# Block 2's scores: a 64-row product for q's low part, or one of 128 rows with zeros

## The chip, the cores and the metric

One core of one Trainium2 chip. The metric is the device time of one launch in microseconds (us). The kernel before was run three times: median 2690.28 us (2690.26, 2690.28, 2696.82).

## The reference

Two transformer blocks, one after the other, on 256 tokens of 1024 features, all in float32. The change touches the attention scores of the second block alone. There each of two layers has 16 heads of 64 features, in two kinds of eight: neighbourhood heads with a relative bias, and windowed heads that share two heads of keys and have a sink. The stream x (256 tokens) looks at its own 256 keys and at the 256 of the context stream c; in layer 0 the context looks at its own 256 keys. Cut to what matters:

```python
s_nb  = einsum('bqhd,biqjhd->bhqij', q_r, k_win) + bias
s_ctx = einsum('bqhd,bchd->bhqc', q_r, k_ctx)
p     = softmax(concatenate([s_nb, s_ctx]))
out   = p_nb @ v_win + p_ctx @ v_ctx
```

## The kernel before, in words

Features lie on the partitions, tokens along the free dimension. Every large product is made in three: weights and activations are split in a high part of 12 significant bits and the exact rest, and high x high, low x high and high x low are added in one bank of PSUM (`feat`, line 161; each weight unit is loaded by DMA, its high part made by ScalarE (ACT), its low part by VectorE (DVE), `weight`, line 140).

One loop (`main`, line 1462) writes the whole program out: it holds threads (the two streams, their attentions, norms) and always lets the one go on whose next step is ready first, by a clock of its own that `mul` (line 109) moves on by the columns of each product, whatever its rows. TensorE (PE) keeps exactly this order. Where a softmax is not done, the other threads' products stand between, so that TensorE has work.

The scores of block 2 come from `attn2` (line 1280). For each head `make` (line 1289) prepares the operands, one head ahead of its use. `keys` (line 840) writes a tile kk of 128 partitions: the head's 64 rows of k, high part, on its own half (from partition kp) and the low part of the same on the other half. `queries` (line 848) writes a tile qq with two planes: the high part of q on both halves (two casts by ACT, line 852), and the low part on the head's own half alone (a subtraction by GpSimd, POOL, line 854); the other half of the second plane holds nothing. The tiles kk and qq have three buffers each.

`unit` (line 1302) is one query tile of 128 for x (512 keys) or both for c (256 keys each); `DEPTH` = 4 units (line 1543) may be open at a time. Its products are listed at line 1319 and made by `rows_of` (line 640, products at line 651, in the profile under line 110):

```python
jobs.append(([(qh, kk), (ql, kk[kp:kp + 64])], b, init, nm[:, hi, qt:qt + 1], sm[:, hi, qt:qt + 1]))
```

The first product of the pair has 128 rows, high q times both parts of k; the second has the 64 rows of the head, low q times high k. Both add into one bank. Then DVE adds the bias and takes the maximum (line 659), ACT takes the exponential (line 665, followed by a read of its accumulator), TensorE turns the tile with four transposes (`turn`, line 669), DVE or ACT copies it (line 292 or 294), and four products with v follow (`values`, line 679). The neighbourhood heads' bias tile is made by `na_bias` (line 1358) with a memset of 128x256 on GpSimd (line 1362).

Of the kernel before, what the change touches and what calls it, by code (L numbers as in the profile page):

```python
# [10 lines left out]
F32 = mybir.dt.float32  # L11
# [5 lines left out]
OP = mybir.AluOpType  # L17
# [4 lines left out]
D = 1024  # L22
# [10 lines left out]
def rows(ap):  # L33
    """[128, n, 256] -> [128, 2n, 128]"""
    return ap.rearrange("p a (b c) -> p (a b) c", c=128)


def back(ap):
    """the same, the 128 tokens of each tile from the last to the first"""
    return rows(ap)[:, :, ::-1]  # L40


class Late:
    """h = a * x * (its tokens' own scales) + b before those scales are there"""
# [9 lines left out]
class Block:  # L54
    """One launch: both blocks of the reference, features on partitions."""
# [42 lines left out]
    def dma(self, out, in_):  # L98
        """in the order of emission, like the work that frees the tiles"""
        self.nc.sync.dma_start(out, in_)  # L100
# [17 lines left out]
    def lat(self, what):  # L118
        """how long it takes until the tensor engine can go on after..."""
        return LAT["x" if self.phase[0] == "x" else "b"][what]  # L120

    def after(self, us):
        """a thread's request to go on once the tensor engine has had this much other work"""
        return ("at", self.clock + us)

# [4 lines left out]
    def fence(self, ins):  # L130
        """later weights are to be split after this"""
        self.fences[ins.ins.engine] = ins.ins
        self.fenced = 0
# [6 lines left out]
    def weight(self, unit):  # L140
        """unit: (input name, leading indices..., first k-tile, k-tiles). (hi, lo), [128, k-tiles, columns] each"""
        if unit in self.store and self.units - self.store[unit][2] <= HELD:
            return self.store[unit][:2]
        src = self.a[unit[0]]
# [8 lines left out]
        # block 1 has the most for DVE to do  # L153
# [7 lines left out]
    def feat(self, out, w, c0, h, hk, first, last, k0=0, k1=None):  # L161
        """out[feature, token] (+)= sum_k w[k, feature] h[k, token], k0 <= k < k1"""
# [10 lines left out]
    def feats(self, name, blocks, h, parts):  # L173
        """one or two blocks of 128 columns into one bank; a generator that returns the bank"""
# [8 lines left out]
    def burst(self, name, pairs, h, emit):  # L183
        """like feats on up to four pairs of blocks, the first of each together, as the tiles of h come.
        emit(which, bank)"""
# [16 lines left out]
    def early(self, name, pairs, late, emit):  # L202
        """like burst, with the tiles of an h that is not normalised yet: late.u. emit(which, banks, columns), a bank for each
        block; the columns [128, 2] are the products with late.u's last two"""
# [41 lines left out]
    def toks(self, name, b, h):  # L246
        """out[token, feature] for 256 columns; a generator that returns the bank"""
# [15 lines left out]
    def rsqrt(self, v):  # L263
        """1/sqrt of a positive float32 tile: a start from the exponent, a step of the third order (times 8/3), one of
        Newton's"""
# [19 lines left out]
    def spread(self, out, col):  # L285
        """out[p, tok] = col[tok] for every p; col [128 tokens, 1]"""
        self.flop(out, col.to_broadcast([128, 128]))
# [15 lines left out]
    def first_h(self, x, cx, units):  # L303
        """the first scale and shift, and h, two feature tiles at a time as the weights of both come"""
# [82 lines left out]
    def affine_split(self, hh, hl, src, k0, a, b):  # L387
        """h = src * a + b on two feature tiles (src [128, 2, 256]); hi and lo"""
# [15 lines left out]
    def add_to(self, key, src, mp, eng):  # L404
        """running sums of feature tiles, two at a time; the last two are kept as they are"""
# [11 lines left out]
    def feed(self, key, x, mp, sums=False):  # L417
        """feature tiles 2 mp and 2 mp + 1 of x are done: add up their squares, and for a LayerNorm their sums"""
# [9 lines left out]
    def total(self, out, tiles):  # L428
        """out[tok] = mean over the partitions and tiles [128, 128 tok]"""
        for i, t in enumerate(tiles):  # L430
            self.mul(out, t, self.ones, i == 0, i == len(tiles) - 1)

    def late_tile(self, late, x, mp):
        """feature tiles 2 mp and 2 mp + 1 of late.u: x times the norm's and the modulation's factors, without the
        tokens' own, which come later"""
# [16 lines left out]
    def ln_shift(self, x):  # L452
        """move the mean of each token's sum so far out of x, so that the variance is well kept"""
# [20 lines left out]
    def ln_late(self, g, b, sh, sc):  # L474
        """what of LN(x) * g + b and h = that * sc + sh is known before x"""
# [9 lines left out]
    def ln_finish(self, key, x, g, b, late=None):  # L485
        """x = LN(x) * g + b, and h = x * late.a + late.b split"""
# [50 lines left out]
    def rms(self, th, x, a, b, late=None):  # L537
        """h = x * rsqrt(mean(x^2) + eps) * a + b, split"""
# [36 lines left out]
    def ffn(self, tags, h, wi, wo, emit, gate, last_gate=None, th=None):  # L575
        """tags: the pages that the product of gate and up may take; a part of seven pages holds six tiles' hi and lo.
        h: hi and lo, or a Late. gate: the event that emit waits for (last_gate, where it is another in the last part).
        emit(parts left, pair, psum) receives each part of the down product"""
# [4 lines left out]
        for i0 in range(0, FT, per):  # L583
# [30 lines left out]
            for mp in range(4):  # L614
# [3 lines left out]
                if late and mp < 2 and len(parts) == 1:  # L618
                    # the last tile of gf is new: it comes last in both
# [20 lines left out]
    def rows_of(self, jobs):  # L640
        """jobs: ([(q, k [.., keys])], additives, start of -max, -max out, sums out), together at most 512 keys wide.
        exp(the sum of q k + additive - max), queries on the partitions"""
# [26 lines left out]
    def turn(self, e):  # L669
        """e [128 q, n keys] -> [128 keys, n / 128, 128 q]"""  # L670
# [12 lines left out]
    def oturn(self, h, osb, k0, scale=None):  # L683
        """osb [128 tokens from the last, 2 halves, 256 features] -> feature tiles k0, k0 + 1 of h; split"""
# [13 lines left out]
    def normed(self, po, sm):  # L698
        """po [128, 2, 4, 64] / sums [128, 4, 2]"""
# [9 lines left out]
    def attend(self, groups, done, gate=None):  # L709
        """A thread. groups: (units, finish); a unit is a generator that yields how long its next step should wait, or  # L710
        that and True when that step has to come in the order of the units; finish, called after the last unit, is a
        generator too, that starts once the event gate has come. done: the event at the end"""
# [45 lines left out]
    def tables(self):  # L758
        """A thread: [head row, 255 - distance] of additive biases, in DRAM, for Toeplitz reads; the differential lambda"""
# [34 lines left out]
    def project(self, name, h, grp, th):  # L794
        """q, k feature-major pages (q scaled, from the last token), v token-major pages"""
# [39 lines left out]
    def causal_jobs(self, q, k, b, nm, sm):  # L835
        """both query tiles of a head: 128 keys, then 256"""
# [3 lines left out]
    def keys(self, k, p0):  # L840
        """k [64 at p0, n]: its hi there, its lo on the other 64 partitions"""
# [6 lines left out]
    def queries(self, q, p0):  # L848
        """q [64 at p0, n]: its hi on all partitions; its lo, [64 at p0, n]"""
# [3 lines left out]
        lo = qq[p0:p0 + 64, 1, :]  # L853
        self.nc.gpsimd.tensor_tensor(out=lo, in0=q, in1=qq[p0:p0 + 64, 0, :].bitcast(F32), op=OP.subtract)
        return qq[:, 0, :], lo

    def attn_diff(self, box):
        """differential heads, two to a group"""
# [54 lines left out]
    def attn_heads(self, grp, box, k0, bias):  # L913
        """eight causal heads, four to a group; bias(head) -> additive [128, 256]"""
# [34 lines left out]
    def forget(self, h):  # L949
        """log_sigmoid(fd + forget_b) and its running sums"""  # L950
# [18 lines left out]
        # log_sigmoid(x) = min(x, 0) - log1p(exp(-|x|)); log1p(e) = ln(u) e / (u - 1), u = 1 + e  # L969
# [13 lines left out]
        # where u == 1, log1p(e) = e to float32; elsewhere ln(u) e / (u - 1)  # L983
# [7 lines left out]
        # running sums with the tokens on partitions, as they come and turned within each tile  # L991
# [17 lines left out]
    def fox_bias(self, hd):  # L1009
        """cum[q] - cum[k], masked to k <= q; queries 0..127 against keys 0..127 sit in columns 128.."""  # L1010
# [89 lines left out]
    def consts1(self):  # L1100
# [7 lines left out]
        # block 1 needs the one, block 2 the other  # L1108
# [9 lines left out]
    def half_out(self, name, o, k0, emit):  # L1118
        """the product with the feature tiles k0 .. k0 + 3 of o"""
# [11 lines left out]
    def consts2(self):  # L1131
# [16 lines left out]
        # q carries the attention scale  # L1148
# [5 lines left out]
    def head_norm(self, tiles, l, done, turned=None):  # L1154
        """A thread. tiles: list of (AP [128, n, 256], gain index, rotary). In place: x * rsqrt(mean over 64 + eps) * g;
        turned: whether their tokens are from the last. done: the event at the end"""
# [56 lines left out]
    def ffn2(self, th, x, l, s, feed, late=None):  # L1213
        """a half step; the squares of its result are summed for the next norm"""
# [19 lines left out]
    def kv(self, th, h, l):  # L1234
        """k (normed, roped) in feature-major pages shared with the other stream, v token-major"""
# [439 lines left out]
```

## Time and profile before

| What | |
|---|---|
| runs | 2690.26, 2690.28, 2696.82 us |
| profiled execution | span 2698.2 us; the page gives no other time of it |
| mean granted TensorE clock | 0.959 |
| TensorE products, busy | 2577.8 us, 96% of the span |
| VectorE (DVE), busy | 1757.5 us, 65% |
| ScalarE (ACT), busy | 1054.8 us, 39% |
| GpSimd (POOL), busy | 224.6 us, 8% |
| chain that ended last | TensorE 77%, DVE 10%, DMA 6% |

How to read it: all times are from the start of the span. PE is TensorE's products, PEld its weight loads, which can run beside products. Matmuls are pipelined, and their ends are modelled, so the distance from one start to the next tells more than a length. A bracket gives an engine's idle time just before an instruction and what ended it; "issue" is time in which it waited for nothing that the profile shows. The granted clock is 1.00 at the full level (2.4 GHz) and 0.50 at the lower one (1.2 GHz).

### The profile page before, as it was taken

Reading aid. Unit: us, or ns where it says so; the run is one execution under the profiler, and the core shown is the slowest. Engines: PE = TensorE matmul, PEld = TensorE weight load, DVE = VectorE, ACT = ScalarE, POOL = GpSimd, SP = SyncE. Lnnn points to the kernel's source line nnn. Section 1 sums busy time; section 2 is a strip of 40 time slices with the busy share of each in tenths; the row PEclk is TensorE's granted clock in tenths of the full one; section 3 lists DMA queues with packets and bytes.
Section 4 is the critical chain, followed back from the end, with each engine's and each line's share of the span. In section 5 each row is a group of like instructions: output and inputs, shape, how many; then the busy total and the mean of one; then the engine's idle time right before and its main releaser. Section 6 shows DMA issues by size and latency. Waiting matters only on the chain.

```text
span 2698.2 us, 49424 instructions
## 1 busy us (share of the span) xinstructions
PE 2577.8 (96%) x20192; PEld 2491.7 (92%) x20192; DVE 1757.5 (65%) x3392; ACT 1054.8 (39%) x1894; POOL 224.6 (8%) x239
## 2 busy tenths in 40 slices
PE   5989998999998999999999999999999999999999
PEld 4879998989998999999888999999999999987999
DVE  6878886678787655676654765656744545675754
ACT  3545444545443222233555322222322223455543
POOL 1111002120000000001431000000000000041000
PEclk9979997979998999999997999999999999989999
DMA  7866884646763444444210244444443444330554
GB/s 279 268 207 211 286 282 154 202 128 199 244 190 111 152 144 139 143 125 133 82 37 32 85 144 132 157 137 138 137 129 118 147 134 127 126 101 32 172 183 139
DMA packets 127396, 410.55 MB, mean 152 GB/s; under 512 B 15617, under 2 KB 21313, under 8 KB 127041
## 3 DMA queue, kind: packets, MB, share of 16 engines
q1 hardware_dynamic: 127168, 407.40, 47.5%
q8 instruction: 158, 2.59, 0.4%
q14 instruction: 70, 0.57, 0.1%
HBM read 406.27 MB, written 1.07 MB: 151 GB/s over the span
## 4 chain that ended last, share of the span: by engine, by line
PE 77%; DVE 10%; DMA 6%; issue 3%; ACT 3%; POOL 1%; SPq 0%; ACTq 0%; DVEq 0%; POOLq 0%
PE ps_mm L110 64%; PE ps_s L110 4%; PE ps_o L110 4%; PE ps_t L115 3%; DVE wl L128 3%; DMA raw<-in_w_ffn_in 2%; PE ps_t L110 2%; DVE junk L376 2%; DMA adaw<-in_w_ada 2%; ACT wh L128 1%; DMA raw<-in_w_ffn_out 1%; DVE x_res L636 1%; DMA raw<-in_w_o 1%; POOL tr L394 0%; DVE tr L563 0%
## 5 line engine op out<-in xcount | busy, mean ns | idle before, releaser
L110 PE MATMUL ps_mm<-hh,wh 128*128 128x256 f32 (+1 forms) x3968 | 1146.6, 289 | 38.7 <-ACT hh L392 23.0
L110 PE MATMUL ps_mm<-hl,wh 128*128 128x256 f32 (+1 forms) x3968 | 1135.9, 286 | 8.0 <-DVE hl L396 4.8
L110 PE MATMUL ps_mm<-hh,wl 128*128 128x256 f32 (+1 forms) x3968 | 1137.0, 287 | 2.1 <-DVE wl L128 2.1
L128 ACT CAST wh<-raw 128x1024 fp32r<-128x1024 f32 (+2 forms) x574 | 547.8, 958 | 756.4 <-PE ps_mm L110 473.8
L110 PEld LDWEIGHTS ps_mm<-hh,wh 128*128 128x128 f32 x3968 | 769.3, 194 | 49.2 <-ACT hh L392 23.4
L128 DVE TENSOR_TENSOR wl<-raw,wh 128x1024 fp32r<-128x1024 f32 (+2 forms) x558 | 627.8, 1129 | 259.3 <-ACT wh L128 256.5
L110 PEld LDWEIGHTS ps_mm<-hl,wh 128*128 128x128 f32 x3968 | 767.8, 193 | 11.9 <-DVE hl L396 5.6
L110 PEld LDWEIGHTS ps_mm<-hh,wl 128*128 128x128 f32 x3968 | 768.6, 194 | 2.6 <-DVE wl L128 2.5
L376 DVE SCALAR_TENSOR_TENSOR junk<-adaw,cb 128x1024 fp8e4<-128x1024 f32 x344 | 426.0, 1238 | 25.2 <-DMA adaw<-in_w_ada 21.6
L110 PE MATMUL ps_mm<-x,wh 128*128 128x256 f32 x1704 | 332.5, 284 | 1.7 <-DVE x_res L636 1.7
L110 PEld LDWEIGHTS ps_mm<-x,wh 128*128 128x128 f32 x1704 | 275.8, 191 | 2.4 <-issue 1.7
L110 PE MATMUL ps_mm<-c,wh 128*128 128x256 f32 x1376 | 269.9, 284 | 3.5 <-ACT c L128 2.2
L595 DVE TENSOR_TENSOR tr<-tr,ps_mm 128x256 f32<-128x256 f32 x189 | 79.3, 420 | 253.8 <-ACT tr L594 252.8
L110 PE MATMUL ps_mm<-x,wl 128*128 128x256 f32 x852 | 241.8, 284 | 1.2 <-DVE wl L128 1.2
L594 ACT ACTIVATE tr<-ps_mm 128x256 f32<-128x256 f32 x189 | 72.6, 384 | 430.2 <-PE ps_mm L110 429.7
L110 PEld LDWEIGHTS ps_mm<-c,wh 128*128 128x128 f32 x1376 | 222.6, 190 | 4.7 <-ACT c L128 2.4
L110 PE MATMUL ps_mm<-c,wl 128*128 128x256 f32 x688 | 194.9, 283 | 1.4 <-DVE wl L128 1.4
L110 PEld LDWEIGHTS ps_mm<-x,wl 128*128 128x128 f32 x852 | 162.7, 191 | 1.4 <-DVE wl L128 1.4
L1187 POOL COPY tr<-small 128x256 f32<-128x256 f32 x44 | 21.0, 507 | 1386.7 <-DVE small L282 1353.2
L110 PEld LDWEIGHTS ps_mm<-c,wl 128*128 128x128 f32 x688 | 130.9, 190 | 1.6 <-DVE wl L128 1.6
L636 DVE SCALAR_TENSOR_TENSOR c_res<-ps_mm,ada_c,c_res 128x256 f32<-128x256 f32 x112 | 49.3, 479 | 93.0 <-PE ps_mm L110 93.0
L665 ACT ACTIVATE e<-e,small 128x512 f32<-128x512 f32 (+2 forms) x160 | 90.7, 568 | 42.9 <-DVE small L659 40.4
(254 smaller groups left out, 2784.9 us busy)
## 6 DMA issues: line engine op xcount, KB each, us to landing
adaw<-in_w_ada SPq DMA_DIRECT2D x232, 512.0 KB, 4.3
raw<-in_w_ffn_up SPq DMA_DIRECT2D x176, 512.0 KB, 3.8
raw<-in_w_ffn_in SPq DMA_DIRECT2D x88, 512.0 KB, 4.5
raw<-in_w_ffn_down SPq DMA_DIRECT2D x96, 384.0 KB, 3.2
raw<-in_w_ffn_out SPq DMA_DIRECT2D x48, 384.0 KB, 3.9
raw<-in_w_in SPq DMA_DIRECT2D x28, 512.0 KB, 3.8
raw<-in_w_in_ab SPq DMA_DIRECT2D x16, 512.0 KB, 6.4
raw<-in_w_o SPq DMA_DIRECT2D x16, 512.0 KB, 4.8
```

The costliest lines, as they stand in the source:

```text
L110: self.tc.keep_in_program_order(self.nc.tensor.matmul(out, left, right, start=start, stop=stop))
L115: self.tc.keep_in_program_order(self.nc.tensor.transpose(out, in_, self.ident))
L128: return (self.nc.scalar.copy(hi, src), (eng or self.nc.vector).tensor_tensor(out=lo, in0=src, in1=hi.bitcast(F32), op=OP.subtract))
L376: ins = self.nc.vector.scalar_tensor_tensor(out=self.junk, in0=raw, scalar=1.0, in1=v, op0=OP.mult, op1=OP.mult, accum_out=acc[:, j:j + 1] ...
L594: nc.scalar.activation(sg[:, 0, :], ps[:, 0, :], AF.Silu)
L595: nc.vector.tensor_tensor(out=sg[:, 1, :], in0=sg[:, 0, :], in1=ps[:, 1, :], op=OP.mult)
L636: self.nc.vector.scalar_tensor_tensor(out=x[:, k, :], in0=ps[j], scalar=gate[:, k:k + 1], in1=x[:, k, :], op0=OP.mult, op1=OP.add)
L665: nc.scalar.activation(e[:, at:at + w], e[:, at:at + w], AF.Exp, bias=nm, scale=-1.0, accum_out=sm)
L1187: nc.gpsimd.tensor_copy(wide, r[:, :, i, :, None].to_broadcast([128, 2, 2, 64]))
```

## The change

`queries` writes zeros to the other half of the second plane, with a memset on GpSimd ahead of the subtraction, and returns the whole plane. The second product of each pair takes all 128 rows of it with the whole of kk: low q times high k on the head's half, zero times low k on the other. Everything else in the diff takes out comments and moves no code.

```diff
     def queries(self, q, p0):
         qq = self.page("qq", (128, 2, q.shape[1]), F32R)
         for p in (p0, 64 - p0):
             self.nc.scalar.copy(qq[p:p + 64, 0, :], q)
-        lo = qq[p0:p0 + 64, 1, :]
-        self.nc.gpsimd.tensor_tensor(out=lo, in0=q, in1=qq[p0:p0 + 64, 0, :].bitcast(F32), op=OP.subtract)
-        return qq[:, 0, :], lo
+        self.nc.gpsimd.memset(qq[64 - p0:128 - p0, 1, :].bitcast(F32), 0.0)
+        self.nc.gpsimd.tensor_tensor(out=qq[p0:p0 + 64, 1, :], in0=q, in1=qq[p0:p0 + 64, 0, :].bitcast(F32),
+                                     op=OP.subtract)
+        return qq[:, 0, :], qq[:, 1, :]
...
     def attn2(self, th, l, box, kind):
...
-                jobs.append(([(qh, kk), (ql, kk[kp:kp + 64])], b, init, nm[:, hi, qt:qt + 1], sm[:, hi, qt:qt + 1]))
+                jobs.append(([(qh, kk), (ql, kk)], b, init, nm[:, hi, qt:qt + 1], sm[:, hi, qt:qt + 1]))
```

## Rows read from the trace of the kernel before

**Rows 1.** The chain of waits, 1290 to 1490 us, its shares by line

```profile
by line: PE ps_mm L110 29.2%; PE ps_o L110 25.0%; PE ps_s L110 23.7%; PE ps_t L115 17.2%; PE ps_t L110 2.7%; DVE e L659 0.7%; DVE junk L376 0.5%; DVE hl L128 0.3%; DVE pt L292 0.3%; issue 0.3%; DVE small L1177 0.1%; DVE small L702 0.1%; DVE
```

**Rows 2.** Windows, all engines: start:end, length, busy us (count), granted clock, DMA

```profile
1300.00:1490.00 190.00, 187.81 (x1158) 159.62 (x1157) 105.54 (x273) 105.24 (x261) 55.04 (x74) 0.86 0.13 41
2390.00:2490.00 100.00, 93.99 (x605) 74.86 (x604) 61.60 (x139) 57.12 (x127) 28.54 (x34) 0.95 0.16 48
```

**Rows 3.** Groups by form, low products and their weight loads: busy, mean; idle, releasers

```profile
L110 PE MATMUL ps_s<-kk,qq 64*128 64x512 f32 x64 | 33.3, 520 | 0.0
...
L110 PEld LDWEIGHTS ps_s<-kk,qq 64*128 64x128 f32 x96 | 19.1, 199 | 21.6 <-issue 18.3 <-POOL tr L1187 0.3 <-POOL qq L854 0.2
...
L110 PE MATMUL ps_s<-kk,qq 64*128 64x256 f32 x32 | 14.2, 443 | 0.0
```

**Rows 4.** Timeline, weight loads (PEld): start, length, instruction, [idle before, releaser]

```profile
1300.80 0.19 PEld L110 LDWEIGHTS ps_s<-kk,qq 128*128 128x128 f32 x1
1301.25 0.18 PEld L110 LDWEIGHTS ps_s<-kk,qq 64*128 64x128 f32 x1 [0.26 <-issue]
1301.67 0.19 PEld L110 LDWEIGHTS ps_s<-kk,qq 128*128 128x128 f32 x1 [0.24 <-issue]
...
1302.53 0.19 PEld L110 LDWEIGHTS ps_mm<-hh,wh 128*128 128x128 f32 x1 [0.25 <-issue]
```

**Rows 5.** Timeline, weight loads in block 1

```profile
95.94 0.52 PEld L110 LDWEIGHTS ps_s<-x,x 64*128 64x128 f32 x4 [0.17 <-issue]
96.79 0.19 PEld L110 LDWEIGHTS ps_mm<-hh,wh 128*128 128x128 f32 x1 [0.33 <-issue]
96.90 0.19 PEld L110 LDWEIGHTS ps_mm<-hh,wl 128*128 128x128 f32 x1
97.02 0.19 PEld L110 LDWEIGHTS ps_mm<-hl,wh 128*128 128x128 f32 x1
```

**Rows 6.** Timeline, weight loads of a c unit, full clock

```profile
1360.26 1.14 PEld L110 LDWEIGHTS ps_s<-kk,qq 128*128 128x128 f32 x4
1361.53 0.75 PEld L115 LDWEIGHTS ps_t<-c_ident,e 128*128 128x128 f32 x7
```

**Rows 7.** Timeline, weight loads at the lower clock level

```profile
1325.55 0.34 PEld L110 LDWEIGHTS ps_s<-kk,qq 128*128 128x128 f32 x1
...
1327.05 0.71 PEld L115 LDWEIGHTS ps_t<-c_ident,tr 128*128 128x128 f32 x4 [0.44 <-issue]
...
1328.17 0.33 PEld L110 LDWEIGHTS ps_mm<-hl,wh 128*128 128x128 f32 x1
1328.39 0.33 PEld L110 LDWEIGHTS ps_mm<-hh,wh 128*128 128x128 f32 x1
...
1446.59 0.33 PEld L110 LDWEIGHTS ps_s<-kk,qq 128*128 128x128 f32 x1
...
1448.68 0.71 PEld L115 LDWEIGHTS ps_t<-c_ident,e 128*128 128x128 f32 x4 [0.22 <-issue]
```

**Rows 8.** Windows: instructions on qq alone, then on ps_mm alone

```profile
1437.00:1474.60 37.60, 13.46 (x24) 7.15 (x24) 4.78 (x12) 4.36 (x6) 0.50 0.03 11
...
1437.00:1474.60 37.60, 5.16 (x24) 5.16 (x24) 0.00 (x0) 0.00 (x0) 0.50 0.03 11
2406.40:2490.00 83.60, 12.96 (x96) 11.78 (x96) 3.50 (x8) 0.00 (x0) 1.00 0.11 33
```

**Rows 9.** Groups by form on GpSimd: memset, subtraction of q's low part

```profile
L854 POOL TENSOR_TENSOR qq<-x,qq 64x256 fp32r<-64x256 f32 x32 | 25.7, 805 | 65.7 <-ACT qq L852 64.7
...
L1362 POOL MEMSET bias<- 128x256 f32 x16 | 5.0, 311 | 26.2 <-DVE small L659 25.9
```

**Rows 10.** Timeline, ACT and weight loads at a turn in layer 1

```profile
2423.61 0.19 ACT L665 ACTIVATION_READ_ACCUMULATOR e<-e,small 128x1 f32 x1
...
2423.93 0.42 PEld L115 LDWEIGHTS ps_t<-c_ident,e 128*128 128x128 f32 x4 [0.24 <-ACT e L665]
```

**Rows 11.** Windows, all engines, where c's units stand close

```profile
1360.00:1380.00 20.00, 18.74 (x131) 15.97 (x130) 10.78 (x32) 15.60 (x43) 6.22 (x8) 1.00 0.08 27
```

## The prediction

> **What bounds the kernel.** I read the chain of waits first, over the stretch of the first attention stage (1290 to 1490 us). It is TensorE nearly throughout: the score products (ps_s) carry 23.7% of it, some 47 of 200 us, and no other engine reaches 1% with any one line [rows 1]. So what TensorE saves here shortens the stage, unless something else comes late. The windows over both attention stages (1300 to 1490 us, layer 0 with both streams; 2390 to 2490 us, layer 1 with x alone) agree: TensorE is busy 187.81 of 190 and 93.99 of 100 us, DVE and ACT 55 to 62% [rows 2]. The groups by form count what the change touches: 64 products of 64x512 and 32 of 64x256, each with a weight load that has 21.6 us of idle time before the 96 of them, nearly all "issue": nothing in the trace is waited for [rows 3].
>
> The weight loads in order of time show what that idle time is. Two score pairs stand between projection products: a full load at 1300.80, a 64-row one at 1301.25, a full one at 1301.67, a 64-row one, and the next projection's load at 1302.53. Each begins 0.24 to 0.26 us after the load before has ended, 0.43 us after that one's start [rows 4]. In block 1 four 64-row loads in succession run without a gap, and the projections' 128-row loads follow each other every 0.12 us; the gap stands only where one kind follows the other (0.17 us going in, 0.33 coming out) [rows 5]. So I take it that a load is hidden behind the running product where both have the same number of rows, and that a change of rows empties the array and exposes the load. Block 2's scores change twice for every low product.
>
> **The change part by part.**
>
> *The low product gets 128 rows.* The columns streamed and the number of loads and products stay the same; the two changes of rows go. A warm pair of 512 columns takes 0.86 us now (1301.67 to 1302.53) [rows 4]. No 512-column product of 128 rows stands between others of its kind in this trace. Nearest is the 256-column one, every 0.12 us [rows 5], doubled 0.24 (an estimate); the ends are 0.21 (512 columns at 2.4 GHz) and 0.43, what each half takes now. I take 0.24, since it is the same engine at the same clock: 0.86 - 2 x 0.24 = 0.38 saved a pair. A warm unit of the c stream is four 256-column products, 1360.26 to 1361.53, 1.27 us [rows 6]; less 4 x 0.12 it saves 0.79. At the lower clock level a 512-column pair takes 1.50 us and a c unit 2.09, and a projection product 0.22 [rows 7]; savings 1.50 - 0.88 = 0.62 and 2.09 - 0.88 = 1.21. In the long stretch at granted clock 0.50, 1437.0 to 1474.6, stand 24 of these products [rows 8], that is five c units and two pairs; all others I price as warm. The sum: 62 pairs x 0.38 = 23.6, 2 x 0.62 = 1.2, 11 units x 0.79 = 8.7, 5 x 1.21 = 6.0, together 39.5 us: 27.3 in layer 0 (30 of the warm pairs) and 12.2 in layer 1.
>
> The rule that speaks against this is in the Trainium skill, "TensorE: Matmul & The Clock Gate", Part 3, "The mechanism": a weight load overlaps a running product only when the two have different row groups. By it two full products could not hide each other's loads either, and the sum would be about 0. The projections' loads, all on the same 128 rows, say otherwise here [rows 5].
>
> *48 memsets on GpSimd*, one ahead of each head's subtraction (32 of x, 16 of c). One of 128x256 takes 0.31 us; for half the partitions nothing smaller is in the trace, and the 64x256 subtraction takes 0.81 [rows 9]. So 15 us of GpSimd time, 39 at most. I cost it at nothing on the path. What hides it: before its 32 subtractions for x GpSimd stood idle 65.7 us, 64.7 of them for ACT's two casts into the same tile [rows 9]; the memset needs the same tile free as the casts, not their result, so it runs while they do, and it blocks nothing that the subtraction behind it didn't block. If that cover fails, the cost is bounded by what TensorE waits for the low part now, 0.2 us before all 96 loads [rows 3]: the operands are made a head ahead. I keep 0 to 5 us (16 c heads x 0.31, these having one unit of lead). A gain is excluded, for nothing is taken from GpSimd.
>
> *The order* of emission is unchanged: `mul` advances its clock by columns, not rows. No DMA is moved.
>
> *What is late next.* TensorE asks earlier for exponentials and copies. In layer 1 a turn's load starts 0.13 us after ACT's accumulator read (2423.61 + 0.19 to 2423.93) and is put down to ACT [rows 10]: there is no room at such places. I give back a third of layer 1's 12.2, 4 us. In 1360 to 1380 us ACT is busy 15.60 of 20 [rows 11]; five c units less there at 0.79 would leave 16.0 us for that work, and ACT next to no idle time: 2 us given back, an estimate. Ends: 0, and half the gross, 20.
>
> Net: 39.5 - 4 - 2 = 33.5, say 34 us. The profiled execution spans 2698.2 us, 7.9 over the median of the runs (2690.28) and 1.4 over the slowest of three (2696.82); its own time around the span isn't told. On it the sum gives 2664; on the median, where I set the forecast, **2656 us**.
>
> **The rivals.**
> 1. *ACT or the latency of the softmax takes over*: half of the gross is given back, 2690 - 20 = 2670 us. For it: rows 10 and 11. Against: both stages still have ACT and DVE near 60% [rows 2], and four units are open at once.
> 2. *The low clock stretch shortens too.* The 37.6 us at 0.50 held 24 projection products, the 83.6 us of layer 1 at clock 1.00 held 96 [rows 8], 0.64 against 1.15 per us. Without the emptying of the array the same products stand closer. The sum already takes 7 us from the stretch (5 x 1.21 and 2 x 0.62). If the clock stays up, the other 30 shrink as 2.09 to 1.27 [rows 6, 7], by 12: 2644 us.
> 3. *Slower: the clock falls where it now holds.* Denser bursts end in waits for exponentials; if layer 1's 83.6 us ran at the low level, they would last as 2.09 to 1.27 [rows 6, 7], 54 us longer: 2656 + 54 = 2710. It decides against the change from about 53 us of warm work on (34 / 0.65). Against: nothing is added to TensorE, and these 83.6 us hold their clock [rows 8].
> 4. *The load stays exposed*: the change gives wide full products, but each load still waits. Then nothing is saved, 2690 us, up to 2695 with the memsets. The block 1 and projection loads speak against it [rows 5]. This is what the rule on row groups (the Trainium skill, the same section) would do here.
>
> **How the numbers follow.** Forecast 0.63, rival 1 0.14, rival 2 0.13, rival 4 0.06, rival 3 0.04. Low end: gross saving with nothing given back and rival 2's gain, 2690 - 40 - 12 = 2638, and 4 more for products at 0.21 (64 pairs x 0.06): 2634. High end: rival 1 with 5 us of memsets, 2675. A measurement of this kernel can tell about 0.3%, 8 us, from no change. Faster by more: the forecast, rivals 1 and 2, less a little for a deeper give-back than half, 0.88. Within it: rival 4 and that remainder, 0.08. Slower: 0.04.
>
> **What would show it.** Right: no 64-row group among block 2's products; the loads of low products without idle time before them, the c units' products 0.12 us apart, a pair under 0.5 us; 48 more memsets of 0.3 to 0.4 us on GpSimd, and TensorE's wait for the low part still under 1 us; layer 0's stage shorter by 25 us or more, layer 1's by about 8. Wrong: loads of 128 rows still 0.24 us late (rival 4); new waits of TensorE for ACT's exponentials above 10 us (rival 1); granted clock 0.50 through most of layer 1's stage (rival 3), or no long stretch of it in layer 0's (rival 2).

## The result: 2647.41 us, and the profile after

| | before | changed |
|---|---|---|
| median of the runs, first comparison | 2693.55 us (2690.26 to 2703.14, 4 runs) | 2647.41 us (2642.82 to 2653.49, 4 runs) |
| ratio, 95% interval | | 0.9836 [0.9806, 0.9865] |
| a second comparison | 2690.24 us (12 runs) | 2647.81 us (4 runs), 0.9839 [0.9809, 0.9868] |
| profiled execution: span, granted clock | 2698.2 us, 0.959 | 2651.4 us, 0.965 |

The change makes the kernel 42 to 46 us faster. The profiled execution of the changed kernel has a time of 2653.49 us, 2.1 more than its span. The spans differ by 46.8 us. Between these two profiles the stretch from one attention stage to the other and the one behind the second moved by at most 0.6 us, and what stands ahead of the first differs by 0.1. All the rest is in the two stages, here taken from the first to the last score product on qq: layer 0 fell from 181.3 to 141.1 us, layer 1 from 91.0 to 85.0.

Windows over these two stages of the kernel before, layer 0, then layer 1. The columns are those of [rows 2]: length, busy us (count) of PE, PEld, DVE, ACT and POOL, granted clock, DMA share, GB/s.

```profile
1300.90:1482.20 181.30, 179.11 (x1085) 151.19 (x1083) 101.49 (x263) 102.13 (x254) 55.04 (x74) 0.85 0.14 42
2393.40:2484.40 91.00, 85.79 (x541) 67.47 (x540) 57.96 (x129) 53.56 (x121) 28.54 (x34) 0.94 0.15 47
```

The same windows of the changed kernel:

```profile
1301.00:1442.10 141.10, 136.46 (x1086) 129.92 (x1085) 101.71 (x263) 100.63 (x254) 64.24 (x104) 0.98 0.18 54
2352.70:2437.70 85.00, 76.36 (x541) 66.52 (x541) 56.94 (x129) 53.52 (x121) 32.14 (x47) 0.94 0.17 53
```

The number of products is the same but for one record, and TensorE's 20192 products stand in the same order in both profiles, by the names of their tiles. Three things differ. TensorE's busy time in layer 0 falls by 42.7 us. The granted clock there rises from 0.85 to 0.98. And TensorE's idle time grows, from 2.2 to 4.6 us in layer 0 and from 5.2 to 8.6 in layer 1.

The groups by form of the changed kernel, which answer to [rows 3]:

```profile
L110 PEld LDWEIGHTS ps_s<-kk,qq 128*128 128x128 f32 x192 | 29.0, 193 | 5.4 <-DVE small L659 3.3 <-ACT qq L852 1.4 <-POOL qq L854 0.2
```

No 64-row load is left among block 2's scores. Of the 21.6 us of idle time before them 18.3 had no releaser [rows 3]; that is gone: the 5.4 us before all 192 loads are put down to engines, to DVE that frees a bank of scores most of all. The wait for the low part of q on GpSimd is still 0.2 us.

The weight loads at the place of [rows 4], in order of time, in the changed kernel, and TensorE's products at the place of the c unit of [rows 6] (start, length, instruction):

```profile
1300.87 0.77 PEld L110 LDWEIGHTS ps_s<-kk,qq 128*128 128x128 f32 x4
1301.69 0.19 PEld L110 LDWEIGHTS ps_mm<-hh,wh 128*128 128x128 f32 x1
```

```profile
1351.20 0.64 PE L110 MATMUL ps_s<-kk,qq 128*128 128x256 f32 x4
1351.68 1.03 PE L115 MATMUL ps_t<-c_ident,e 128*128 128x128 f32 x8
```

The four loads of two pairs now follow each other without a gap, 0.82 us from the first to the next projection's load where there were 1.73 [rows 4]. The c unit's four products take 0.48 us, 0.12 each, where the same unit took 1.27 by its loads [rows 6]. It stands behind a projection; most units stand behind narrower products and take 0.56, as told below.

Groups by form on GpSimd in the changed kernel, which answer to [rows 9]:

```profile
L854 POOL TENSOR_TENSOR qq<-x,qq 64x256 fp32r<-64x256 f32 x32 | 25.7, 803 | 11.2 <-ACT qq L852 9.8
L853 POOL MEMSET qq<- 64x256 f32 x48 | 14.7, 306 | 88.0 <-PE ps_s L110 85.2 <-ACT hh L128 2.3
```

The memsets take 0.31 us each, 14.7 in all, the same for 64 partitions as for 128. GpSimd's idle time has moved from the subtraction (65.7 us ahead of x's before, 11.2 now) to the memset, which waits until TensorE has read the tile; then it runs ahead of ACT's casts or beside them.

### The profile page after: what moved, and what is told of

Its sections match the earlier page's. It is cut to its first block, busy times and chain, and to the rows that moved or that the text cites. A ratio compares the mean times of both kernels' runs of the same rounds, so it can differ in the third digit from the quotient of the medians.

```text
span 2651.4 us, 49490 instructions
## 1 busy us (share of the span) xinstructions
PE 2529.3 (95%) x20192; PEld 2473.8 (93%) x20192; DVE 1760.6 (66%) x3392; ACT 1053.7 (40%) x1894; POOL 239.4 (9%) x287
## 4 chain that ended last, share of the span: by engine, by line
PE 77%; DVE 10%; DMA 6%; ACT 3%; issue 3%; POOL 1%; SPq 0%; ACTq 0%; DVEq 0%; POOLq 0%
PE ps_mm L110 65%; PE ps_s L110 3%; PE ps_o L110 3%; DVE wl L128 3%; PE ps_t L115 3%; DVE junk L376 2%; PE ps_t L110 2%; DMA raw<-in_w_ffn_in 2%; DMA adaw<-in_w_ada 2%; ACT wh L128 1%; DMA raw<-in_w_ffn_out 1%; DVE x_res L636 1%; DMA raw<-in_w_o 1%; POOL tr L394 1%; DVE tr L563 0%
## 5 line engine op out<-in xcount | busy, mean ns | idle before, releaser
L110 PEld LDWEIGHTS ps_mm<-hh,wh 128*128 128x128 f32 x3968 | 770.0, 194 | 46.9 <-ACT hh L392 24.1
```

Source lines behind the costliest of these rows:

```text
L110: self.tc.keep_in_program_order(self.nc.tensor.matmul(out, left, right, start=start, stop=stop))
```

## The experiments

The theory: a change between 64 and 128 rows costs TensorE time at every switch, and this time is what the change saves. The first rival: the saving comes from something else that the change brings, the memset or the order of writes. The second: the lower clock level. Two corrections are used with every run, and stand here once. A unit of the c stream lasts 2.09 us at clock 0.50 where it lasts 1.27 at 1.00 [rows 6, 7], so that one us at 0.50 costs 1 - 1.27/2.09 = 0.39 us. (The 29 runs of the kernel before that stood beside the first four experiments give 0.33 by themselves, as the slope of their spans against their us at 0.50; the 12 and the 11 that stood beside the later ones give 0.40 and 0.41.) The granted clock of each execution has two levels, so that a mean of g over a span of S us means 2 x (1 - g) x S us at 0.50. The stages' us at 0.50 are summed from the trace's record of the clock.

**1. The memset alone.** The kernel differs from the changed one in this line.

```diff
-jobs.append(([(qh, kk), (ql, kk)], ...
+jobs.append(([(qh, kk), (ql[kp:kp + 64], kk[kp:kp + 64])], ...
```

> The 48 memsets alone; the low products keep their 64 rows. Theory (what counts is the change of rows; the memsets run while ACT casts): no difference, within 4 us of the kernel before, and GpSimd busy 15 us longer. Rival (the memsets delay the low part, and the gain of the change is net of that): up to 15 us slower, with TensorE waits for GpSimd's low part of several us.

Measured: 2691.0 us (10 runs), before 2686.77 (29 runs), ratio 1.0013 [0.9997, 1.0029]. The memset neither helps nor costs anything that shows, as the theory had it (the interval leaves room for 8 us of cost, and none of help above 1): the rows of the product do it.

**2. Half the changes of rows, in c alone.** In the kernel before, the second query tile of a c unit takes its low product first, so that the unit has two products of 64 rows in succession.

```diff
-jobs.append(([(qh, kk), (ql, kk[kp:kp + 64])], ...
+pair = [(qh, kk), (ql, kk[kp:kp + 64])]
+jobs.append((pair[::-1] if th == "c" and qt == 1 else pair, ...
```

> The kernel before, with the second pair of each c unit turned round: high, low, low, high, so that two 64-row products follow each other. No memset, and every low product keeps its 64 rows. Theory (the cost is in the change of rows): the load of the second low product is hidden, two of four changes go, 0.4 us less of each of 16 warm c units (0.6 at the lower clock), 6 to 8 us less in all; up to 12 more if the long stretch at granted clock 0.50 goes with them. Rival (a 64-row product is slow by itself): the same c unit of 1.27 us and no difference.

Measured: 2680.19 us (12 runs), ratio 0.9974 [0.9953, 0.9996], 7 us faster, within the theory's 6 to 8; but about half of that is the clock, and corrected for it the mean span is 3.6 us shorter, the stage in the profile 5.2 (tables below). The trace shows the saving itself. The weight loads of the unit of [rows 6] in this kernel, four in one line, of which the middle two have 64 rows:

```profile
1347.96 0.94 PEld L110 LDWEIGHTS ps_s<-kk,qq 128*128 128x128 f32 x4
1348.84 0.45 PEld L115 LDWEIGHTS ps_t<-c_ident,e 128*128 128x128 f32 x4
```

From the unit's first load to the next group's it is 0.88 us, where it was 1.27. The second 64-row load starts 0.11 us after the first, with no idle time before it; the two loads at which the rows change still have 0.13 and 0.14 us. Nothing but the order of two products differs; rows, columns and loads are the same. So the price hangs on the change of rows, not on 64 rows as such.

**3. The change in layer 1 alone**, and the memset under the same condition.

```diff
+low = (ql, kk) if l == 1 else (ql[kp:kp + 64], kk[kp:kp + 64])
-jobs.append(([(qh, kk), (ql, kk)], ...
+jobs.append(([(qh, kk), low], ...
```

> The change in layer 1 alone; layer 0 keeps the 64-row products and has no memset. Theory (layer 1 gives 12 us gross and returns about half of it in waits for DVE and ACT; the rest of the gain is layer 0's, its clock included): 5 to 8 us faster than before, and layer 0's scores end at the same time as before, with its stretch at 0.50. Rival (the extra gain over the forecast lies in layer 1): 15 us faster or more.

Measured: 2675.92 us (12 runs), ratio 0.9973 [0.9957, 0.9989]. The difference of the medians is 10.9 us, by the ratio 7, the theory's 5 to 8; corrected, the mean span is 4.9 us shorter. Layer 0's stage, corrected, is as long as before (table below); it had 34 us at 0.50, with a stretch of 10.2 at its end.

**4. One more look at the kernel before**, for what differs between two executions of the same kernel.

> A second profile of the kernel before. Theory (the long stretch at granted clock 0.50 in layer 0 belongs to this kernel's density of products): again 30 us or more at 0.50 between 1430 and 1480 us. Rival (it is chance of that one execution): no stretch of more than 10 us there, and the time some 12 us shorter.

Measured: 2685.03 us. Its long stretch at clock 0.50 at the end of layer 0 lasts 20.5 us, not 37.6, between the theory's 30 and the rival's 10. The whole stage has 47.8 us at 0.50, not 54.6, and there are 119.5 ahead of it, not 139.9. So the clock differs between executions of one kernel, and a sum against one profile carries that.

**5 and 6. The change for x alone, and for c alone** (the condition of experiment 3 with `th == "x"`, then `th == "c"`), **and the changed kernel again.**

> The change for the x stream's units alone (64 pairs, both layers); c's units keep the 64-row products. Theory (each stream gives its own changes of rows): layer 0's scores last some 10 us less than before at the same time at granted clock 0.50, layer 1's 6 us less, 15 to 20 us in all; the stretch at 0.50 where c's units end layer 0's stage is still there, 15 us or more. Rival (the clock part comes with any part of the change): the stretch is gone and the gain is 25 us or more.

> The change for the c stream's units alone (16 units, layer 0); x's units keep the 64-row products. Theory: layer 0's scores last some 11 us less than before at the same time at granted clock 0.50, and the stretch at 0.50 among c's last units is mostly gone, 8 to 12 us more; layer 1 as before: 15 to 23 us faster. Rival (the clock has nothing to do with the c units): 11 us.

> A second profile of the changed kernel, and its runs on the same chip as the others. Theory (without the changes of rows TensorE's products stand closer and the clock holds): less than 20 us at granted clock 0.50 within layer 0's scores, which last 140 to 146 us; 38 to 44 us faster than before. Rival (the first profile had a lucky clock): 30 us or more at 0.50, layer 0's scores over 150 us, and about 28 us faster than before.

Measured, beside 2690.24 us before (12 runs): x alone 2661.44 us, 0.9892 [0.9869, 0.9915]; c alone 2666.16, 0.9923 [0.9894, 0.9952]; both 2647.81, 0.9839 [0.9809, 0.9868]. By the medians 28.8, 24.1 and 42.4 us: the two parts make more than the whole, and each gave more than its theory (15 to 20, and 15 to 23). x alone gave what its rival said, 25 or more, but not for the rival's reason: its profile still has a stretch of 17.1 us at 0.50 where c's last units stand. The changed kernel came out as its theory had it. What clears the rest is the clock. The table takes every comparison's runs, with the mean of their spans and of their granted clocks, and takes 0.39 us off for each us at 0.50.

| kernel (runs) | mean span | mean clock | us at 0.50 | span, corrected |
|---|---|---|---|---|
| before (12) | 2688.1 | 0.9609 | 210 | 2606.2 |
| memset alone (10) | 2688.3 | 0.9610 | 210 | 2606.5 |
| half the changes in c (12) | 2677.9 | 0.9635 | 196 | 2601.6 |
| layer 1 alone (12) | 2676.1 | 0.9637 | 195 | 2600.3 |
| c alone (7) | 2667.5 | 0.9657 | 183 | 2596.1 |
| x alone (6) | 2660.0 | 0.9653 | 184 | 2588.1 |
| changed (4) | 2645.6 | 0.9677 | 171 | 2579.0 |

(Before has 2605.2 in the 29 runs that stood beside the first four kernels.) Corrected, the parts add up, within an uncertainty of 1 to 2 us: 18.1 for x and 10.1 for c make 28.2, both together 27.2. The rest of the 42.5 us, 15, is (210 - 171) x 0.39: fewer us at the lower clock. This part doesn't add up: x alone has 10 us of it and c alone 11.

The stages of the profiled executions tell the same. Windows over layer 0's stage with the change in c alone, in x alone, and in both (the second profile):

```profile
1290.70:1446.30 155.60, 151.53 (x1085) 133.16 (x1084) 102.97 (x263) 101.22 (x254) 59.89 (x90) 0.95 0.16 49
```

```profile
1286.10:1447.00 160.90, 158.23 (x1085) 142.44 (x1084) 101.46 (x263) 101.45 (x254) 59.59 (x88) 0.90 0.16 47
```

```profile
1285.10:1428.00 142.90, 138.07 (x1085) 131.32 (x1084) 102.82 (x263) 100.52 (x254) 64.36 (x104) 0.96 0.18 53
```

| execution | layer 0: us, at 0.50, corrected | layer 1: us, at 0.50, corrected |
|---|---|---|
| before | 181.3, 54.6, 160.0 | 91.0, 10.2, 87.0 |
| before, again | 178.2, 47.8, 159.6 | 91.3, 10.2, 87.3 |
| memset alone | 172.1, 30.7, 160.1 | 96.8, 23.9, 87.5 |
| layer 1 alone | 173.5, 34.1, 160.2 | 86.7, 13.7, 81.4 |
| half the changes in c | 166.8, 30.7, 154.8 | 107.2, 51.2, 87.2 |
| x alone | 160.9, 30.7, 148.9 | 85.5, 10.2, 81.5 |
| c alone | 155.6, 17.1, 148.9 | 91.1, 10.2, 87.1 |
| changed | 141.1, 6.8, 138.4 | 85.0, 10.2, 81.0 |
| changed, again | 143.0, 10.2, 139.0 | 86.7, 13.7, 81.4 |

One factor, taken from two rows of the trace, brings executions with the same products together within 0.6 us in a stage, where their lengths differ by 9 us (layer 0, 64-row products in both streams) and 16 us (layer 1, 64-row products). Layer 0 saves 21 us, 11.1 with either stream; layer 1 saves 5.8. Half the changes of rows in c save 5.2 us, nearly half of c's 11.1. The us at 0.50 in layer 0 mostly go along with the rows: 31 to 55 with the 64-row product in both streams, 17 and 31 with it in one, 3 to 10 with it in neither and the same order of products (experiment 7 among these). But the two executions of experiments 8 and 9, with it in neither and another order, have 27 and 17, so the rows alone don't set it. What goes along with c's rows is the long stretch, the longest at 0.50 in the last 50 us of the stage: 10 to 38 us in the five executions with c's 64-row products as they were (17.1 with x alone), 17.1 with half their changes, 0 to 7 in the six with none. Each of these is one execution, and why the throttle grants what it does in a stretch isn't settled by these runs.

**7. The same for block 1.** Its scores are products of 64 rows among products of 128 [rows 5]. Beside the change, each head's q is copied there with zeros in the other half (a memset and a copy on GpSimd, one head ahead), and multiplied with the whole tile of k.

```diff
-q, k = self.head_ops(res, hd)
+q, k = made[hd]
...
+qz = self.page("qq", (128, 2, 256), F32R)[:, 0, :].bitcast(F32)
+self.nc.gpsimd.memset(qz[64 - p0:128 - p0, :], 0.0)
+self.nc.gpsimd.tensor_copy(qz[p0:p0 + 64, :], q)
```

> The changed kernel, and block 1's 32 heads as well: q copied by GpSimd beside zeros into a tile of 128 rows, one head ahead, and multiplied with the full 128 rows of k. Theory (each 64-row group costs about 0.5 us of exposed loads, 0.17 going in and 0.33 coming out, where TensorE bounds the stage): 32 groups x 0.5 = 16 us at most, 5 to 12 us faster than the changed kernel. Rival (block 1's attention waits for DVE, ACT and DMA, and GpSimd comes late with the copies): within 4 us of the changed kernel, or slower.

Measured: 2631.51 us (2628.47 to 2636.46, 4 runs), ratio to the kernel before 0.9781 [0.9753, 0.9808], 16 us under the changed kernel beside it: the fastest version of this study, and beyond the theory's 5 to 12. The loads of block 1's scores, groups by form, in the second profile of the changed kernel and then in this one:

```profile
L110 PEld LDWEIGHTS ps_s<-c,c 64*128 64x128 f32 x64 | 9.1, 203 | 2.0 <-issue 0.7 <-DVE wl L128 0.2
L110 PEld LDWEIGHTS ps_s<-x,x 64*128 64x128 f32 x64 | 8.2, 194 | 2.1 <-issue 0.8 <-DVE junk L376 0.3
```

```profile
L110 PEld LDWEIGHTS ps_s<-x,qq 128*128 128x128 f32 x64 | 9.4, 209 | 0.1
L110 PEld LDWEIGHTS ps_s<-c,qq 128*128 128x128 f32 x64 | 8.4, 191 | 0.0
```

The idle time before these 128 loads went from 4.1 to 0.1 us. But little of the gain is that. The mean span is 2630.2 us at a mean clock of 0.9735, that is 139 us at 0.50 and 2575.9 us corrected, only 3.1 under the changed kernel's 2579.0, with an uncertainty near 2; the other 12 are 32 us less at the lower clock. So the theory's reason is borne out at a smaller size, and its total only by way of the clock, for which it gave no reason.

**8 and 9. A later turn.** Where did part of the saving go? The planner (`mul`) counts 0.43 us for a pair of 512 columns, which took 0.83 at the full clock before and takes 0.54 now; so its delays, counted on that clock, have become shorter in true time. The changed kernel with `LAT["x"]` raised, "soft" from 2.7 to 3.1 and "turn" from 1.4 to 1.6, then to 3.6 and 1.8:

```diff
-'soft': 2.7, 'split': 1.9, 'turn': 1.4
+'soft': 3.1, 'split': 1.9, 'turn': 1.6
```

> The changed kernel with the planner's delays in block 2's attention longer: from the scores to the turn 3.1 us instead of 2.7, from the turn to the products with v 1.6 instead of 1.4. It asks where layer 1's saving went: its stage (first to last score product, low-clock time taken out at 0.39 us per us) fell from 87.2 to 81.4 us, 5.8 of the 12.2 forecast before giving back. Theory A: the planner counts 0.43 us for a pair of 512 columns that took 0.86 in the kernel before and takes 0.47 now, so its delays were longer in true time than written and are now as short as written; TensorE comes too early. Then this run shortens layer 1's stage, so corrected, to 78 to 80 us, TensorE's waits there for the exponential, the copy and the scores' maximum fall from 8.8 us to 4 to 7, and the time is 2642 to 2646. Rival B: with two PSUM buffers for scores and two for turns, the chain score, maximum, exponential, turn is what fills the stage; a later turn holds the buffers no shorter, the waits change names only, the stage stays at 81 to 82 and the time at 2645 to 2650. Rival C: with four units open, a later turn starves the start of new units: stage over 83, time over 2651.

> The same edit doubled: 3.6 us from the scores to the turn, 1.8 from the turn to the products with v. Theory A: the waits that are left are gone or nearly so, stage of layer 1 at 77 to 80 us, time as in the run before or up to 3 us less, since four open units set an end to it. Rival B: stage 81 to 82, time 2645 to 2650. Rival C: stage 84 or more and slower than the run before by 3 us or more.

Measured: 2658.73 us, 0.988 [0.9845, 0.9916], and 2666.12 us, 0.9911 [0.9877, 0.9945]: slower than the changed kernel (0.9839) by about 11 and 18. Windows over both stages of the first:

```profile
1291.50:1464.00 172.50, 156.91 (x1165) 148.80 (x1164) 104.48 (x273) 105.21 (x261) 63.47 (x106) 0.92 0.15 44
2362.60:2445.50 82.90, 75.27 (x533) 65.99 (x533) 56.35 (x128) 53.54 (x121) 33.90 (x47) 0.94 0.18 54
```

Layer 1's stage, corrected, is 79.0 us, as theory A said, but with 8 products fewer in it, and TensorE's idle time there only fell from 8.6 to 7.6 us. In layer 0, where 79 more products now stand in the stage, it rose from 4.6 to 15.6: the new order ran into other waits (its longest, 3.2 us, before a score product for ACT's casts into qq). Theory A is refuted as a way to win time, and as the reason of the waits in layer 1 it is not shown. In the second run layer 1's stage is 92.7 us with 17.1 at 0.50, 86.0 corrected, which is rival C's number; in the first, rival C was right in the total and not in the place.

## Why the prediction was right, and where its sum was not

The forecast of 2656 us was 9 over the measured time, within the range and on the right side. That it came so near is in part luck: a saving sized too large and a gain from the clock that the forecast nearly left out stood against each other. Point by point:

**The mechanism** was right. The change of rows exposes the load, and with 128 rows in both products it is hidden (the loads of 1300.87; experiments 1 and 2). That the array is emptied at the change is the prediction's picture of it; the runs show the exposed load alone. Rival 4, the rule on row groups of the Trainium skill ("TensorE: Matmul & The Clock Gate", Part 3, "The mechanism"), read without the exception that the section itself makes for a background weight buffer, is refuted here: 192 loads on the same rows as the product that runs have no exposed gap. Another page of the Trainium skill, "TensorEngine Tiling (Array Packing)", Key Properties, says that changing the tiling mode drains TensorE. This case's traces fit that: a pair that loses its changes gets 0.30 us shorter.

**The saving of a pair was mis-sized.** The step "A warm pair of 512 columns takes 0.86 us now" and so "0.38 saved a pair" took a pair that stands behind another pair, and the c unit one behind a projection. Two pairs of layer 1 in the kernel before, one behind projections, one behind transposes:

```profile
2449.38 0.82 PE L110 MATMUL ps_s<-kk,qq 128*128 128x512 f32 x2
2450.14 1.09 PE L115 MATMUL ps_t<-c_ident,e 128*128 128x128 f32 x8
2450.98 0.91 PE L110 MATMUL ps_s<-kk,qq 128*128 128x512 f32 x2
2451.83 0.38 PE L110 MATMUL ps_mm<-hh,wh 128*128 128x256 f32 x1
2452.05 0.28 PE L110 MATMUL ps_mm<-hh,wl 128*128 128x256 f32 x1
```

and the same two in the changed kernel:

```profile
2406.39 0.63 PE L110 MATMUL ps_s<-kk,qq 128*128 128x512 f32 x2
2406.85 1.04 PE L115 MATMUL ps_t<-c_ident,e 128*128 128x128 f32 x8
2407.64 0.71 PE L110 MATMUL ps_s<-kk,qq 128*128 128x512 f32 x2
2408.19 0.28 PE L110 MATMUL ps_mm<-hh,wh 128*128 128x256 f32 x1
2408.32 0.28 PE L110 MATMUL ps_mm<-hh,wl 128*128 128x256 f32 x1
```

From one start to the next the first pair went from 0.76 to 0.46 us, the second from 0.85 to 0.55: each saves 0.30, not 0.38. Only a pair behind another saves 0.39. Behind transposes or products of 64 columns the first of a pair still takes some 0.31 us to the next start; that the narrow products ahead don't cover its load is how I read it, and wasn't tried. Over all pairs at the full clock that no wait follows, the mean went from 0.83 to 0.54 us (51), and only 9 of the 51 are under 0.5 us, which the prediction had named as a sign. The mean of a c unit went from 1.22 (11) to 0.57 (14), 0.65 saved and not 0.79.

The product right behind a pair changes too: it took 0.22 us to the next start (2451.83 to 2452.05) and takes 0.13 (2408.19 to 2408.32). Adding up both stages from one start to the next, with TensorE's idle time in a row of its own and 0.39 us taken off for each us at 0.50, shows where the time went, before and changed:

| us | layer 0 | layer 1 |
|---|---|---|
| the pairs of x (32 in each layer) | 26.1, 17.2 | 25.6, 17.3 |
| the 16 units of c | 19.6, 9.4 | |
| the first product behind a pair or unit (44 and 25) | 7.9, 4.7 | 4.4, 3.0 |
| all other products (912 and 451) | 104.2, 102.5 | 51.8, 52.1 |
| TensorE's idle time | 2.2, 4.6 | 5.2, 8.6 |
| sum, the corrected stage | 160.0, 138.4 | 87.0, 81.0 |

The first three rows save 22.3 us in layer 0 (0.34 a pair and 0.71 a unit, with the products behind them) and 9.7 in layer 1 (0.30 a pair): 32.0 us. The forecast's prices at the full clock, 64 x 0.38 and 16 x 0.79, make 37.0.

**What is given back was sized right.** TensorE's idle time grew by 3.4 us in layer 1 (4 were forecast) and by 2.4 in layer 0 (2 were forecast). The other products make 1.4 us less, of which the correction for the clock can be a part: in the second profile of the kernel before they have 103.7 in layer 0. TensorE's waits in layer 1's stretch, before (2340 to 2490 us; what waited, for what: us, times, longest):

```profile
PE ps_o L110 <- DVE pt L292: 1.2, 1, 1.2
...
PE ps_o L110 <- ACT pt L294: 0.4, 1, 0.4
PE ps_s L110 <- DVE small L659: 0.3, 1, 0.3
PE ps_t L115 <- ACT e L665: 0.3, 1, 0.3
```

and in the changed kernel:

```profile
PE ps_s L110 <- DVE small L659: 2.5, 3, 1.1
...
PE ps_o L110 <- DVE pt L292: 1.3, 1, 1.3
...
PE ps_t L115 <- ACT e L665: 0.9, 3, 0.5
PE ps_o L110 <- ACT pt L294: 0.8, 1, 0.8
```

Most of the new wait is not ACT's, as rival 1 and rows 10 had it, but that for a bank of scores that DVE's maximum (line 659) must free: 2.2 of the 3.4 us. The waits for ACT's exponential and for its copy grew by 0.4 us each within the stage. The second profile of the changed kernel has the same three waits. The 20 us that rival 1 gave back did not come.

**The memsets** cost nothing on the path that can be told: in experiment 1 the corrected mean span is 2606.5 us beside 2605.2, with a standard deviation of 3 us in either set of runs (10 and 29).

**Rival 2 was not a rival but a part of the sum.** It had a chance of 0.13 and a price of 12 us; the runs give 15. In the profile, layer 0 went from 54.6 to 6.8 us at 0.50, and (54.6 - 6.8) x 0.39 = 18.6 us of its 40.2 are the clock. The stretch of 37.6 us [rows 8] is gone. The forecast's sum had 2.5 us of this: its prices at the low level, 7.2 us for five units and two pairs, are that much over the prices at the full one. So two errors stood against each other. At the full clock the forecast's sum is 37.0 - 6 = 31 us, and the runs give 27; the clock gave 15 where the sum had 2.5. Without the clock the time would have been some 7 us above the forecast; with it, it is 9 below. Rival 3, a fall of the clock in layer 1, did not come: 10.2 us at 0.50 before and after, 13.7 in the second profile after.

## What to carry to other kernels

A product on half of the array's rows between products on all of them costs more than its columns: price it from one start to the next in the trace, at every kind of place where it stands, not at one, and take in the product right behind it. Zeros in the unused half and a full product are cheaper, if the memset has an idle engine; where that can't be, put the products of the same height next to each other. And separate the clock from the rest: the span and the mean granted clock of every run together show which part of a gain is fewer cycles and which is a higher clock.

## What was not expected

- The time of one kernel varies by 18 us between its runs (2679.98 to 2698.23 in 29 runs of the kernel before) and by 30 in another set (2676.32 to 2706.35 in 11). Half of the variance in the first set and nine tenths in the second is the clock: with 0.39 us taken off for each us at 0.50, the standard deviation of the spans falls from 4.7 to 3.4 us, and from 8.5 to 2.4.
- A change that takes out few us of work can go with many by the clock: the runs with block 1's full products have some 3 us of work less and 32 us less at the lower level, worth 12. Why the clock held there isn't shown.
- Part of the price of a change of rows stands in the product behind it, which took 0.07 us longer to the next start on the mean of both stages.
- A memset of 64x256 takes as long as one of 128x256, 0.31 us.
